# ReLU and row mean over 16384 rows: the last row in its own tile, and the program written with its own semaphores

## The chip, the cores and the metric

The kernel runs on one core of one Trainium2 chip. The metric is the device time of one execution in microseconds (us). The profile comes from one such execution. Engines are named as in the profile: DVE is VectorE, ACT is ScalarE, POOL is GpSimd, PE is TensorE (not used for work here), SP is SyncE, which issues the transfers. A letter q behind a name means the engine's sequencer, which handles waits and semaphores.

## The reference

The input x is float32 of shape 32 x 512 x 1024. Each value is replaced by max(x, 0), and the mean over the last axis is returned, as float32 of shape 32 x 512:

```python
relu_x = np.maximum(x, 0)
return np.mean(relu_x, axis=-1).astype(np.float32)
```

So there are 16384 rows of 1024 values. 67.11 MB are read and 64 KB are written.

## The kernel before

The rows are laid over the 128 partitions, 128 consecutive rows (index j from 0 to 127) to a partition. A tile `xt` holds 16 of a partition's rows: 64 KB per partition, 8 MB in all. The pool `in` has three such buffers. Seven full tiles are loaded with one transfer each (line 92). The eighth is loaded in smaller parts: row pieces of 8, 4, 2 and 1 rows (line 100), and then its last row, j = 127, in column pieces of 512, 256 and 256 columns (line 104). All transfers are issued by SP, and all go through one queue in that order.

The function `rows` gives each row to an engine: even rows to ACT, odd rows to DVE. `act_row` (line 15) is one activation with the function Relu, whose accumulated sum goes to a column of `sums`. `dve_row` (line 20) is one tensor_scalar, max with 0 and an accumulated sum; it can begin the sum with a value of its own (`init`). In the profile each of the two shows as two instructions, the main one and a read of the accumulator. `finish` (line 85) lets POOL multiply a range of `sums` by 1/1024 into `res`.

The end of the work is written out one by one. Row 126 (`prev`) is split in halves between ACT and DVE, and POOL joins and scales the two sums (line 118). The last row (`last`) lies in the same tile as the rest. Its first piece is split between ACT and DVE; POOL scales ACT's part (line 123). Its second piece is split likewise, where DVE's sum goes on from the one before (`init`), and ACT adds and scales its part (line 128). DVE alone takes the third piece, again going on from its sum, and then joins the two sides (line 132). SP stores `res` with one transfer (line 135).

The order on each engine is the order of the calls. What waits for what is worked out by the tile framework: it gives semaphores to engines and transfers, and eight of them are shared in turn by the transfers, so that a later transfer waits for the earlier one with the same semaphore. `tc.close()` (line 139) ends the tile context. At that place SP waits for the transfers' semaphores, all engines meet, POOL clears the semaphores, and all engines meet again. The function `issue_ahead_of_entry_barrier` then moves the first load in front of the meeting of all engines at the program's start (line 155 in the profile).

Of the kernel before, what the change touches and what calls it, by code (L numbers as in the profile page):

```python
# [1 line left out]

# [4 lines left out]

F32 = mybir.dt.float32
ALU = mybir.AluOpType
ACT = mybir.ActivationFunctionType  # L10


def act_row(nc, src, acc):

    nc.scalar.activation(out=src, in_=src, func=ACT.Relu, accum_out=acc)  # L15


def dve_row(nc, src, acc, init=None):

    nc.vector.tensor_scalar(  # L20
        out=src, in0=src, scalar1=0.0, scalar2=init,
        op0=ALU.max, op1=ALU.add, accum_out=acc,
    )


def issue_ahead_of_entry_barrier(nc):


    entry, body = nc.cur_f.blocks[0].instructions, None
    for block in nc.cur_f.blocks[1:]:  # L30
        for k, ins in enumerate(block.instructions):
            if ins.opcode == "DMACopy":
                body, load = block.instructions, k
                break
        if body is not None:
            break
    first = body[load]
    assert first.engine == mybir.EngineType.SP and not first.sync_info.on_wait
    assert all(i.opcode == "DMACopy" or i.engine != first.engine for i in body[:load])
    del body[load]  # L40
    at = next(k for k, i in enumerate(entry) if i.engine == first.engine and i.opcode == "Drain")
    entry.insert(at, first)


@with_exitstack
def kernel(
    ctx: ExitStack,
    tc: tile.TileContext,
    x: bass.AP,
    out: bass.AP,  # L50
):
    nc = tc.nc
    P = nc.NUM_PARTITIONS
    xf = x.flatten_outer_dims()
    R, D = xf.shape
    assert R % P == 0
    J = R // P
    inv = 1.0 / D
    xr = xf.rearrange("(p j) d -> p j d", p=P, j=J)
    outr = out.flatten().rearrange("(p j) -> p j", p=P, j=J)  # L60
    xlast = xr[:, J - 1, :]

    NB = 16
    full = J // NB - 1

    row_pieces = [8, 4, 2, 1]
    assert sum(row_pieces) == NB - 1
    col_pieces = [512, 256, 256]
    assert sum(col_pieces) == D

    pools = ctx.enter_context(ExitStack())
    in_pool = pools.enter_context(tc.tile_pool(name="in", bufs=3))
    res_pool = pools.enter_context(tc.tile_pool(name="res", bufs=1))
    sums = res_pool.tile([P, J], F32)
    res = res_pool.tile([P, J], F32)
    part = res_pool.tile([P, 10], F32)

    def rows(xt, lo, n, j0):

        for k in range(lo, lo + n):  # L80
            j = j0 + k
            (dve_row if j % 2 else act_row)(nc, xt[:, k, :], sums[:, j:j + 1])

    def finish(lo, hi):
        nc.gpsimd.tensor_scalar(  # L85
            out=res[:, lo:hi], in0=sums[:, lo:hi], scalar1=inv, scalar2=0.0, op0=ALU.mult, op1=ALU.add,
        )

    for t in range(full):
        j0 = t * NB  # L90
        xt = in_pool.tile([P, NB, D], F32, name="xt")
        nc.sync.dma_start(out=xt, in_=xr[:, j0:j0 + NB, :])  # L92
        rows(xt, 0, NB, j0)

    j0 = full * NB
    xt = in_pool.tile([P, NB, D], F32, name="xt")
    prev, last = xt[:, NB - 2, :], xt[:, NB - 1, :]
    lo = 0
    for n in row_pieces:
        nc.sync.dma_start(out=xt[:, lo:lo + n, :], in_=xr[:, j0 + lo:j0 + lo + n, :])  # L100
        lo += n
    c = 0
    for w in col_pieces:
        nc.sync.dma_start(out=last[:, c:c + w], in_=xlast[:, c:c + w])
        c += w

    finish(0, j0)
    lo = 0
    for n in row_pieces[:-1]:
        rows(xt, lo, n, j0)  # L110
        lo += n
    finish(j0, j0 + lo)

    act_row(nc, prev[:, :512], part[:, 0:1])
    dve_row(nc, prev[:, 512:], part[:, 1:2])
    nc.gpsimd.tensor_scalar(  # L118
        out=res[:, J - 2:J - 1], in0=part[:, 0:1], scalar1=part[:, 1:2], scalar2=inv, op0=ALU.add, op1=ALU.mult,
    )  # L120
    act_row(nc, last[:, :256], part[:, 2:3])
    dve_row(nc, last[:, 256:512], part[:, 3:4])
    nc.gpsimd.tensor_scalar(  # L123
        out=part[:, 4:5], in0=part[:, 2:3], scalar1=inv, scalar2=0.0, op0=ALU.mult, op1=ALU.add,
    )
    act_row(nc, last[:, 512:640], part[:, 5:6])
    dve_row(nc, last[:, 640:768], part[:, 6:7], init=part[:, 3:4])
    nc.scalar.activation(  # L128
        out=part[:, 7:8], in_=part[:, 5:6], func=ACT.Identity, scale=inv, bias=part[:, 4:5],
    )  # L130
    dve_row(nc, last[:, 768:], part[:, 8:9], init=part[:, 6:7])
    nc.vector.scalar_tensor_tensor(  # L132
        out=res[:, J - 1:J], in0=part[:, 8:9], scalar=inv, in1=part[:, 7:8], op0=ALU.mult, op1=ALU.add,
    )
    nc.sync.dma_start(out=outr, in_=res)

    pools.close()
    tc.close()
    tc.compile()
    issue_ahead_of_entry_barrier(nc)  # L140


# [1 line left out]
_INS = ['x']  # L144
_OUTS = [((32, 512), 'float32')]


# [23 lines left out]
```

## Time and profile before

| what | value |
|---|---|
| median of 20 runs | 164.0 us (163.61 to 164.39) |
| profiled execution, device time | 164.39 us |
| its span, first to last instruction | 162.6 us |
| DVE busy | 74.7 us (46%), 135 instructions |
| ACT busy | 69.6 us (43%), 134 instructions |
| POOL busy | 1.2 us (1%), 8 instructions |
| HBM read | 67.11 MB, 413 GB/s over the span |

The span runs from the first instruction of the kernel to its last, and the device time of the same execution is 1.79 us longer. The busy times are sums over the whole span. The waits of the sequencers and the transfers aren't in them, so the last few microseconds are read from the chain of waits and from the engines' timelines.

### The profile page before, as it was taken

The numbers are of one execution on the slowest core, as the hardware profiler recorded it, in microseconds if no ns is written. First come the engines' busy times: TensorE is split into PE (matmuls) and PEld (weight loads), VectorE is DVE, ScalarE is ACT, GpSimd is POOL, SyncE is SP. The second block draws the span as 40 slices with busy tenths as digits, with TensorE's granted clock in tenths as the row PEclk, the third lists the DMA queues.
The fourth block names the chain that finished last, engine by engine and source line by source line (L and its number), as shares of the span: only waits on it lengthen the run. The fifth ranks groups of instructions, "written<-read, shape, count | busy, mean of one in ns | idle before, by whom it ended". The sixth has DMA issues, their size and how long they took to land.

```text
span 162.6 us, 358 instructions
## 1 busy us (share of the span) xinstructions
DVE 74.7 (46%) x135; ACT 69.6 (43%) x134; POOL 1.2 (1%) x8
## 2 busy tenths in 40 slices
DVE  0000059700795009930099201990049800698993
ACT  3000059500793009910099001980049600696882
POOL 0000000000000000000000000000000000000001
DMA  7998997997998998998998998998999997999980
GB/s 258 516 468 355 468 516 322 451 516 339 435 516 355 419 516 371 403 468 387 435 486 373 435 484 371 435 500 371 419 500 419 403 484 339 427 435 403 407 310 17
DMA packets 2162, 67.19 MB, mean 413 GB/s; under 512 B 240, under 2 KB 624, under 8 KB 880
## 3 DMA queue, kind: packets, MB, share of 16 engines
q1 hardware_dynamic: 2160, 67.18, 96.4%
q14 instruction: 2, 0.02, 0.0%
HBM read 67.11 MB, written 0.07 MB: 413 GB/s over the span
## 4 chain that ended last, share of the span: by engine, by line
DMA 84%; DVE 13%; SPq 1%; issue 0%; DVEq 0%
DMA xt<-in_x_dram 84%; DVE xt L20 12%; SPq L100 1%; DVE res L132 0%; DVEq L20 0%; SPq L92 0%; DVEq L132 0%
## 5 line engine op out<-in xcount | busy, mean ns | idle before, releaser
L20 DVE TENSOR_SCALAR_CACHE_REDUCE xt<-xt 128x1024 f32<-128x1024 f32 (+1 forms) x65 | 73.6, 1194 | 85.2 <-DMA xt<-in_x_dram 84.9
L15 ACT ACTIVATE xt<-xt 128x1024 f32<-128x1024 f32 (+1 forms) x66 | 67.0, 1016 | 89.2 <-DMA xt<-in_x_dram 89.1
L15 ACT ACTIVATION_READ_ACCUMULATOR xt<-xt 128x1 f32 x66 | 12.3, 186 | 0.0
L20 DVE DVE_READ_ACCUMULATOR xt<-xt 128x1 f32 x65 | 5.3, 82 | 0.0
L85 POOL TENSOR_SCALAR res<-sums 128x112 f32<-128x112 f32 (+1 forms) x2 | 0.5, 252 | 157.2 <-DVE xt L20 157.2
L15 ACT ACT_TABLE_LOAD x1 | 1.3, 1283 | 0.8 <-PEq L155 0.8
L20 DVE TENSOR_SCALAR_CACHE_REDUCE xt<-xt,part 128x128 f32<-128x128 f32 (+1 forms) x2 | 0.8, 412 | 0.1
L128 ACT ACTIVATE part<-part 128x1 f32<-128x1 f32 x1 | 0.3, 294 | 0.1
L118 POOL TENSOR_SCALAR res<-part 128x1 f32<-128x1 f32 x1 | 0.3, 264 | 0.5 <-ACT xt L15 0.5
L132 DVE SCALAR_TENSOR_TENSOR res<-part 128x1 f32<-128x1 f32 x1 | 0.2, 160 | 0.1
L123 POOL TENSOR_SCALAR part<-part 128x1 f32<-128x1 f32 x1 | 0.2, 191 | 0.1
L20 DVE DVE_READ_ACCUMULATOR xt<-xt,part 128x1 f32 x2 | 0.2, 82 | 0.0
L155 POOL MEMSET const-bfloat16-1.0<- 128x1 bf16 x1 | 0.1, 101 | 0.0
L155 POOL MEMSET const-uint8-127<- 128x1 uint8 x1 | 0.1, 101 | 0.0
L155 POOL MEMSET const-float32-0.0<- 128x1 f32 x1 | 0.1, 98 | 0.2 <-issue 0.2
L155 POOL MEMSET const-float32-1.0<- 128x1 f32 x1 | 0.1, 98 | 0.0
## 6 DMA issues: line engine op xcount, KB each, us to landing
xt<-in_x_dram SPq DMA_DIRECT2D x1, 4096.0 KB, 39.0
xt<-in_x_dram SPq DMA_DIRECT2D x1, 2048.0 KB, 43.5
xt<-in_x_dram SPq DMA_DIRECT2D x1, 1024.0 KB, 45.5
xt<-in_x_dram SPq DMA_DIRECT2D x1, 512.0 KB, 46.4
xt<-in_x_dram SPq DMA_DIRECT2D x1, 256.0 KB, 46.5
xt<-in_x_dram SPq DMA_DIRECT2D x2, 128.0 KB, 42.7
xt<-in_x_dram SPq DMA_DIRECT2D x7, 49.4
out_dram<-res SPq DMA_DIRECT2D x1, 64.0 KB, 1.5
```

The source lines that it names most:

```text
L15: nc.scalar.activation(out=src, in_=src, func=ACT.Relu, accum_out=acc)
L20: nc.vector.tensor_scalar(out=src, in0=src, scalar1=0.0, scalar2=init, op0=ALU.max, op1=ALU.add, accum_out=acc,)
L85: nc.gpsimd.tensor_scalar(out=res[:, lo:hi], in0=sums[:, lo:hi], scalar1=inv, scalar2=0.0, op0=ALU.mult, op1=ALU.add,)
L100: nc.sync.dma_start(out=xt[:, lo:lo + n, :], in_=xr[:, j0 + lo:j0 + lo + n, :])
L118: nc.gpsimd.tensor_scalar(out=res[:, J - 2:J - 1], in0=part[:, 0:1], scalar1=part[:, 1:2], scalar2=inv, op0=ALU.add, op1=ALU.mult,)
L123: nc.gpsimd.tensor_scalar(out=part[:, 4:5], in0=part[:, 2:3], scalar1=inv, scalar2=0.0, op0=ALU.mult, op1=ALU.add,)
L128: nc.scalar.activation(out=part[:, 7:8], in_=part[:, 5:6], func=ACT.Identity, scale=inv, bias=part[:, 4:5],)
L132: nc.vector.scalar_tensor_tensor(out=res[:, J - 1:J], in0=part[:, 8:9], scalar=inv, in1=part[:, 7:8], op0=ALU.mult, op1=ALU.add,)
L155: nc = _bacc.Bacc("TRN2", target_bir_lowering=False, num_devices=1)
```

## The change

The program is no longer written within the tile framework. The tile context is closed at the top of the function, when it is still empty, so its two meetings of all engines stand at the start of the program. Buffers are allocated by name, and every wait and count is written by hand: each of the 14 loads has a semaphore of its own, and the engines count in three further ones (`act`, `dve`, `pool`). Loads, their sizes and their order are the same, and so is the work on rows 0 to 125. After the store SP clears the semaphores, waits for the store, and the program ends there.

Row 126 is split at column 448 instead of 512. The last row has a tile of its own with 1026 columns. ACT takes the whole first piece and writes its sum into column 1024; DVE takes the second piece and writes its sum into column 1025. One scalar_tensor_tensor on DVE then runs over columns 768 to 1025, that is the third piece and the two sums: max with 0, times 1/1024 from the tile `scale` (filled by POOL at the start), and the accumulated sum goes straight into `res`. The two sums aren't negative, so max leaves them as they are.

```diff
+    tc.close()
+    tc.compile()
...
+    last = sbuf("last", P, D + 2)
+    scale = sbuf("scale", P, D // 4 + 2)
+
+    loaded = [nc.alloc_semaphore(f"loaded{i}") for i in range(full + len(row_pieces) + len(col_pieces))]
+    act, dve, pool = (nc.alloc_semaphore(n) for n in ("act", "dve", "pool"))
+    stored = nc.alloc_semaphore("stored")
+
+    def load(i, dst, src):
+        nc.sync.dma_start(out=dst, in_=src).then_inc(loaded[i], 16)
+
+    def buf_free(t):
+        if t >= BUFS:
+            nc.sync.wait_ge(act, t - BUFS + 1)
+            nc.sync.wait_ge(dve, t - BUFS + 1)
+
+    for t in range(full):
+        buf_free(t)
+        load(t, bufs[t % BUFS][:, :, :], xr[:, t * NB:(t + 1) * NB, :])
...
+    nc.gpsimd.memset(scale[:, :], inv).then_inc(pool, 1)
+
+    def rows(i, xt, lo, n, j0):
+        nc.scalar.wait_ge(loaded[i], 16)
+        nc.vector.wait_ge(loaded[i], 16)
         for k in range(lo, lo + n):
             j = j0 + k
-            (dve_row if j % 2 else act_row)(nc, xt[:, k, :], sums[:, j:j + 1])
+            done = (dve_row if j % 2 else act_row)(nc, xt[:, k, :], sums[:, j:j + 1])
+            if k >= lo + n - 2:
+                done.then_inc(dve if j % 2 else act, 1)
...
-    act_row(nc, prev[:, :512], part[:, 0:1])
-    dve_row(nc, prev[:, 512:], part[:, 1:2])
+    nc.scalar.wait_ge(loaded[i], 16)
+    act_row(nc, prev[:, :448], part[:, 0:1]).then_inc(act, 1)
+    nc.vector.wait_ge(loaded[i], 16)
+    dve_row(nc, prev[:, 448:], part[:, 1:2]).then_inc(dve, 1)
...
-    act_row(nc, last[:, :256], part[:, 2:3])
-    dve_row(nc, last[:, 256:512], part[:, 3:4])
-    nc.gpsimd.tensor_scalar(
-        out=part[:, 4:5], in0=part[:, 2:3], scalar1=inv, scalar2=0.0, op0=ALU.mult, op1=ALU.add,
-    )
-    act_row(nc, last[:, 512:640], part[:, 5:6])
-    dve_row(nc, last[:, 640:768], part[:, 6:7], init=part[:, 3:4])
-    nc.scalar.activation(
-        out=part[:, 7:8], in_=part[:, 5:6], func=ACT.Identity, scale=inv, bias=part[:, 4:5],
-    )
-    dve_row(nc, last[:, 768:], part[:, 8:9], init=part[:, 6:7])
+    nc.scalar.wait_ge(loaded[i + 1], 16)
+    act_row(nc, last[:, :512], last[:, D:D + 1]).then_inc(act, 1)
+    nc.vector.wait_ge(loaded[i + 2], 16)
+    dve_row(nc, last[:, 512:768], last[:, D + 1:D + 2]).then_inc(dve, 1)
+    nc.vector.wait_ge(act, n_done + 1)
+    nc.vector.wait_ge(dve, n_done + 1)
+    nc.vector.wait_ge(loaded[i + 3], 16)
     nc.vector.scalar_tensor_tensor(
-        out=res[:, J - 1:J], in0=part[:, 8:9], scalar=inv, in1=part[:, 7:8], op0=ALU.mult, op1=ALU.add,
-    )
-    nc.sync.dma_start(out=outr, in_=res)
-
-    pools.close()
-    tc.close()
-    tc.compile()
+        out=last[:, 768:], in0=last[:, 768:], scalar=0.0, in1=scale[:, :], op0=ALU.max, op1=ALU.mult,
+        accum_out=res[:, J - 1:J],
+    ).then_inc(dve, 1)
+
+    nc.sync.wait_ge(pool, 2)
+    nc.sync.wait_ge(dve, n_done + 2)
+    nc.sync.dma_start(out=outr, in_=res[:, :]).then_inc(stored, 16)
+
+    nc.sync.sem_clear(range(used[0], used[-1] + 1))
+    nc.sync.wait_ge(stored, 16).then_inc(stored, -16)
```

In the built program the waits that stand directly in front of an instruction are merged into it as far as one wait fits; the rest stays as one wait instruction ahead of it. In front of the last DVE instruction that leaves one wait instruction (for the third piece and for DVE's own count) and one wait in the instruction itself (for ACT's count).

## The prediction

> **What bounds the kernel now.** I read the chain of waits first, because it says what the end waited for.
>
> ```profile
> DMA 84%; DVE 13%; SPq 1%; issue 0%; DVEq 0%
> DMA xt<-in_x_dram 84%; DVE xt L20 12%; SPq L100 1%; DVE res L132 0%; DVEq L20 0%; SPq L92 0%; DVEq L132 0%
> q1 hardware_dynamic: 2160, 67.18, 96.4%
> ```
>
> The load stream is the bound: its queue keeps the 16 DMA engines busy for 96.4% of the span, and the DVE steps inside the chain (two stretches of 9.21 us that free a buffer) are passed with two other tiles in flight. So an edit counts only if it moves the stream's start, the stream itself, or what follows its last byte. The end of the chain in order of time shows what follows:
>
> ```profile
> 111.48 46.36 DMA xt<-in_x_dram
> ...
> 157.86 1.07 DVE xt L20 x4
> 158.93 0.02 issue
> 158.96 0.23 DVE xt L20
> 159.18 0.04 issue
> 159.23 0.09 DVE xt L20
> 159.32 0.03 issue
> 159.34 0.50 DVE xt L20 x2
> 159.84 0.03 issue
> 159.87 0.02 DVEq L132
> 159.89 0.05 issue
> 159.94 0.16 DVE res L132
> ```
>
> Row 126 has landed at 157.84. From there five dependent DVE steps run to 160.10: half of row 126, three slices of the last row, one step that joins the halves. The last row's pieces were issued at 111.96, 112.44 and 120.11 and took 46.5, 46.4 and 39.0 us to land; the trace's landing events are 158.47, 158.81 and 159.13. DVE therefore ends 0.97 us after the last byte. What follows is on SP, in its waits:
>
> ```profile
> SPq L135 <- DVE res L132: 39.7, 1, 39.7
> SPq L139 <- DMA out_dram<-res: 1.1, 1, 1.1
> SPq L139 <- PEq L139: 0.6, 2, 0.4
> ```
>
> The store is issued at 160.17 and lands 1.55 us later, at 161.71. Then comes line 139, the exit of the tile context:
>
> ```profile
> L139 SPq EVENT_SEMAPHORE  x6: 17/28/28, 160.6 to 162.5; - x6
> L139 SPq DRAIN  x3: 7/7/7, 161.9 to 162.2; - x3
> L139 POOLq EVENT_SEMAPHORE_RANGE_CLEAR  x1: 95/95/95, 162.2 to 162.2; - x1
> ```
>
> SP checks its remaining DMA semaphores, all engines meet, POOL clears semaphores, all meet again; the last wait ends at 162.61, 0.90 us after the store landed. So three stages lie behind the stream: compute 0.97, store 1.61 with its 0.06 of hand-over, exit 0.90.
>
> [...]
>
> **The change, part by part.**
>
> *Start.* The first load stays ahead of the entry meeting. The exit's two meetings now stand before the remaining loads. The pair took 0.69 us at the end (161.92 to 162.61), so SP's second load moves from 0.77 to about 1.4 us and its third from 1.15 to about 1.9; ACT's 1.28 us table load, POOL's constant fill (new; I allow 1 us) and DVE's wait for it move likewise. The cover is the first 8 MB load, which lands at 22.33: cost nothing, 0.7 us without that cover.
>
> *Stream.* The seven tiles, four row pieces and three column pieces have the same sizes and order, all on SP's queue. Each load has its own semaphore, so the wait in front of the last column piece (7.2 us in SP's waits, to 120.11) is gone; that piece was still queued for 39 us, so it gains nothing. Buffers come free by the same two counts, issued at 31.6 to 110.2 as now, with the next tile already moving. Cost zero. [...] the streams keep nearly the same length (DVE 77 to 72 program instructions in the body), so two fetches stay. [...]
>
> *Row 126.* DVE takes 576 columns instead of 512. From 686 ns at 512 and 1215 at 1024 (1.03 ns a column) that is 752 ns, and the next instruction can start 75 ns before its end: 157.86 + 0.68 = 158.54. ACT takes 448: between 416 at 256 and 629 at 512 this is 576, free at 158.44. POOL's join (0.26 us) follows by about 159.0, and only SP's store waits for it.
>
> *Last row.* ACT takes the whole first piece (512): lands 158.47, starts 158.49, 629 ns, its accumulator read ends 94 ns after (as at 158.40 + 0.19 now), at 159.21. DVE takes the second piece (256): lands 158.81, starts 158.84, 420 ns, read over at 159.26. Then DVE waits for ACT's sum, for its own and for the third piece (159.13). Line 132 now started 0.112 us after the sum before it was written, through one extra wait instruction; the changed program has one there too: start 159.37. Behind it on DVE is nothing, and SP waits for it.
>
> *The final instruction*, 258 columns with accumulation. [...] I take 0.43: the one-source rows with accumulation run at 1.03 ns a column[...]. Its accumulator read adds 10 ns beyond its end: 159.81. It replaces the two slices with their chained starts, ACT's and POOL's scaling, and the join.
>
> *Store.* SP starts 0.064 us after (160.103 to 160.167 now): 159.87 instead of 160.17, a gain of 0.29 us. Landing 1.55 later: 161.42.
>
> *Exit.* SP clears the semaphores during the store's flight (POOL's clear took 95 ns; the cover is about 1.1 us; without it 0.1 us) and waits for the store: 0.016 until the wait sees it, 0.028 for the wait. End 161.46. Gain here 0.85 us.
>
> Sum: 162.61 − 0.29 − 0.85 = 161.46, so −1.15 us. The profiled execution was 164.39 in all, 1.79 more than its span; with that kept it becomes 163.24. It was the slowest of the 20 runs; the same saving from the median gives 164.0 − 1.15 = **162.85 us**. A difference of 0.2%, 0.33 us, is about what a measurement of this kernel can tell from none.
>
> **Rivals.**
>
> *The final instruction at half throughput.* [...] It costs 0.27: 163.12.
>
> *More than I count.* The 1.79 us outside the span shrink, since four engines leave early and only SP comes last, or the instruction fetches fall on a DMA engine with slack. Worth about 0.35: 162.50. Against: whatever waits for all engines still waits for SP.
>
> *The exit meeting isn't really removed.* [...] only the 0.29 of the tail is left: 163.71, just inside 0.2%. For: [...] the time outside the span isn't in the profile. [...] This is also the case in which the change doesn't do what it says.
>
> *Slower.* The last row's new tile starts at an SBUF address that is a multiple of 32 but not of 64 bytes, by the built program; the old rows started on multiples of 64. If such writes are slow, all packets of the last three pieces are: per engine 8 of 84 ns and 16 of 46 ns, 1.41 us. The final instruction has 0.18 us of slack on the third piece, so at r times the cost the end moves by 1.41(r−1) − 0.18. It cancels the gain at r = 1.94 and is slower by 0.2% from r = 2.2; at 2.4, say, 164.6. Against: packets here cost 8 ns plus 38 ns a KB from 1 KB to 64 KB, with no trace of an edge penalty.
>
> **How the numbers follow.** Main case 0.60, half throughput 0.13, more than counted 0.09, exit repaid 0.10, slower 0.08. The first three are faster by over 0.2%: 0.82; within 0.10; slower 0.08. The range takes in those three, 162.50 to 163.12, with 0.2 below and, for medians that differ between sets and a fetch on the wrong engine, 0.4 above: 162.3 to 163.5, with 0.18 left out.
>
> **What would show it.** Right: a span of about 161.5; no meetings after the store; the last instruction is SP's wait, some 0.05 us behind the landing; the final DVE instruction at about 0.43 us, starting about 0.11 us after DVE's second-piece sum; the third piece still landing 1.3 us after row 126; second load near 1.4 us and the first tile's landing unmoved. Wrong: a final instruction near 0.7; third piece later than 1.5 us after row 126; a span shorter by 1.15 with the time unmoved, which would mean the time outside the span grew; or a lower stream rate between 20 and 140 us.

## The result, and the profile after

The changed kernel takes 162.38 us (median, 162.03 to 162.58) against 163.95 us of the kernel before (median, 163.61 to 164.39). The ratio is 0.9902, with a 95% interval of 0.9892 to 0.9912. The change makes the kernel faster by 1.57 us, about 1%. The forecast was 162.85 us within 162.3 to 163.5.

The profiled execution took 162.53 us, its span 161.19 us. So two things became shorter: the span, by 1.42 us against the profiled execution of before (162.61), and the time outside the span, from 1.78 to 1.34 us. Over several executions of each kernel the same split shows with less chance in it (35 of the kernel before, beside the first experiment, and 8 of the changed kernel; spans are on record to 0.1 us):

| median over the executions | kernel before | changed kernel | difference |
|---|---|---|---|
| span | 162.10 us (161.8 to 162.6) | 161.05 us (160.7 to 161.2) | 1.05 |
| device time less span | 1.79 us (1.74 to 1.84) | 1.34 us (1.28 to 1.39) | 0.45 |

The load stream is still the bound. These are lines of the page of the changed kernel; the lower two have packets, MB and the share of the 16 DMA engines.

```profile
span 161.2 us, 336 instructions
...
q1 hardware_dynamic: 2160, 67.18, 97.3%
q14 instruction: 2, 0.02, 0.0%
```

The chain that ended last says little here: on this page it holds only the final DVE instruction. The last event of the program is now SP's own wait for the store, and the chain loses its thread there. The DVE timeline (start, length, then the instruction) shows the end of the compute:

```profile
157.59 0.75 DVE L20 TENSOR_SCALAR_CACHE_REDUCE rows<-rows 128x576 f32<-128x576 f32 x1
158.27 0.08 DVE L20 DVE_READ_ACCUMULATOR rows<-rows 128x1 f32 x1
158.58 0.42 DVE L20 TENSOR_SCALAR_CACHE_REDUCE last<-last 128x256 f32<-128x256 f32 x1 [0.23 <-DMA last<-in_x_dram]
158.93 0.08 DVE L20 DVE_READ_ACCUMULATOR last<-last 128x1 f32 x1
159.11 0.43 DVE L165 SCALAR_TENSOR_TENSOR last<-last,scale 128x258 f32<-128x258 f32 x1
159.46 0.08 DVE L165 DVE_READ_ACCUMULATOR last<-last,scale 128x1 f32 x1
```

DVE is done with its part of row 126 before the second piece has landed and idles for 0.23 us in front of it. The final instruction takes 0.43 us and starts 0.10 us after the sum of the second piece is written (159.01). ACT's timeline shows the first piece, whose sum is ready before that:

```profile
158.23 0.63 ACT L15 ACTIVATE last<-last 128x512 f32<-128x512 f32 x1
158.77 0.19 ACT L15 ACTIVATION_READ_ACCUMULATOR last<-last 128x1 f32 x1
```

The third piece landed at 158.89 (by the trace's landing events), so DVE ended 0.65 us behind the last byte, where the old chain needed 0.97. What follows is in SP's waits:

```profile
SPq L172 <- DVE last L165: 46.5, 1, 46.5
SPq L178 <- SPq L178: 1.1, 1, 1.1
SPq L55 <- PEq L55: 0.5, 2, 0.3
```

The store goes out at 159.62 and lands at 161.16; SP's wait for it (line 178) ends at 161.19, and so does the program. The two meetings of line 55 are at the start now: SP's last wait in them ends at 1.36 us, and its second load goes out at 1.42. The first tile landed at 22.31 (22.33 before).

From the last landing to the end of the span it was 162.61 − 159.13 = 3.48 us before and is 161.19 − 158.89 = 2.30 us now. The difference, 1.17 us before rounding, stands against the 1.15 of the forecast. That the last byte came 0.24 us earlier in this execution is left for the first experiment.

### The profile page after: what moved, and what is told of

It reads as the page before. It is cut to its first block, busy times and chain, and to the rows that moved or that the text cites. A ratio compares the mean times of both kernels' runs of the same rounds, so it can differ in the third digit from the quotient of the medians.

```text
span 161.2 us, 336 instructions
## 1 busy us (share of the span) xinstructions
DVE 74.3 (46%) x132; ACT 69.2 (43%) x131; POOL 1.3 (1%) x8
## 5 line engine op out<-in xcount | busy, mean ns | idle before, releaser
L20 DVE TENSOR_SCALAR_CACHE_REDUCE rows<-rows 128x1024 f32<-128x1024 f32 x64 | 73.4, 1208 | 84.9 <-DMA rows<-in_x_dram 84.7
L15 ACT ACTIVATE rows<-rows 128x1024 f32<-128x1024 f32 x64 | 66.2, 1036 | 88.3 <-DMA rows<-in_x_dram 88.2
L15 ACT ACTIVATION_READ_ACCUMULATOR rows<-rows 128x1 f32 x64 | 12.0, 187 | 0.0
L20 DVE DVE_READ_ACCUMULATOR rows<-rows 128x1 f32 x64 | 5.3, 83 | 0.0
L15 ACT ACTIVATE last<-last 128x512 f32<-128x512 f32 x1 | 0.6, 630 | 0.0
```

What stands on the lines that cost most here:

```text
L15: return nc.scalar.activation(out=src, in_=src, func=ACT.Relu, accum_out=acc)
L20: return nc.vector.tensor_scalar(out=src, in0=src, scalar1=0.0, scalar2=init, op0=ALU.max, op1=ALU.add, accum_out=acc,)
```

## The experiments

My theory after the result: three separate savings, the tail (0.29 us), the exit within the span (0.85) and 0.45 outside the span, which comes from four engines leaving early. The rivals: the last saving belongs to the tail, or to something else in the exit; or the stream itself became faster. Each experiment had the kernel before run beside it. "Outside" is the device time less the span, the median over the executions.

### The kernel before once more

No edit.

> The kernel before once more, for the spans of several of its executions. Both theories: 163.95. If the 0.24 us by which the last piece landed earlier in the changed kernel's trace (158.89 against 159.13) is chance, spans here scatter from about 161.9 to 162.6 around 162.2, and the last landing lies around 158.9. If the hand-written program makes the stream itself faster, the spans stay at 162.5 or more. The time outside the span should be 1.79 in each execution.

Measured: 163.86 us, ratio 1.0000 (0.9991 to 1.0009), spans of 161.8 to 162.5 with a median of 162.10, outside 1.77. In the profiled execution, of 162.1 us, the last piece landed at 158.61, not 159.13. So the profiled execution of before had a late stream by chance, and the 0.24 us aren't owed to the change. Its trace shows where it fell behind: eight 64 KB packets that start between 64.7 and 65.6 us took 2.9 to 3.2 us instead of 2.42. What slowed them is open. The forecast, which took its steps from that execution and its saving from the median, was not harmed by it.

### The new tail alone

The kernel before, within the tile framework and with its exit, but with the new end of the work:

```diff
+    last = res_pool.tile([P, D + 2], F32)
+    scale = res_pool.tile([P, D // 4 + 2], F32)
+    nc.gpsimd.memset(scale, inv)
...
+    act_row(nc, last[:, :512], last[:, D:D + 1])
+    dve_row(nc, last[:, 512:768], last[:, D + 1:D + 2])
+    nc.vector.scalar_tensor_tensor(
+        out=last[:, 768:], in0=last[:, 768:], scalar=0.0, in1=scale, op0=ALU.max, op1=ALU.mult,
+        accum_out=res[:, J - 1:J],
+    )
```

> The kernel before with only the new end of the work: row 126 split at 448, the last row in its own tile, one final DVE instruction; still within the tile framework, with its exit. My theory (three separate savings: tail, exit, outside): 0.22 to 0.29 us less, since the final instruction gets two further waits here, so about 163.7 with 1.79 outside the span. Rival (the new tail is what shortens the time outside the span too, because ACT and POOL stop earlier): about 163.25.

Measured: 163.60 us, ratio 0.9985 (0.9977 to 0.9993), so 0.28 us less; outside 1.79, as before. The DVE timeline of this kernel shows where a part of the saving stays behind:

```profile
158.50 0.08 DVE L20 DVE_READ_ACCUMULATOR last<-last 128x1 f32 x1
158.79 0.43 DVE L126 SCALAR_TENSOR_TENSOR last<-last,scale 128x258 f32<-128x258 f32 x1 [0.21 <-DVE last L20]
```

The framework puts two wait instructions in front of the final instruction, and it starts 0.21 us after the sum before it, twice what one wait instruction takes in the changed kernel. From the last landing (158.46) to the end of the span it is 3.26 us, against 3.48: a saving of 0.21 us before rounding. With the waits of the changed kernel (0.10 us in place of 0.21) it would be 0.11 more. The tail is worth what the forecast gave it, and the rival that ties the outside time to it falls.

### The new program alone

The changed program with the old end of the work, waits written by hand:

```diff
-    last = sbuf("last", P, D + 2)
+    last = xt[:, NB - 1, :]
...
+    act_row(nc, last[:, :256], part[:, 2:3]).then_inc(act, 1)
+    dve_row(nc, last[:, 256:512], part[:, 3:4]).then_inc(dve, 1)
...
+    dve_row(nc, last[:, 640:768], part[:, 6:7], init=part[:, 3:4]).then_inc(dve, 1)
...
+    dve_row(nc, last[:, 768:], part[:, 8:9], init=part[:, 6:7]).then_inc(dve, 1)
```

> The changed program with the old end of the work: row 126 split at 512, the last row in its 8 MB tile and in slices, ACT's and POOL's scaling and the join. My theory: the exit's 0.85 us in the span and 0.45 outside it go, the tail stays: 163.95 - 1.30 = 162.65, with 1.34 outside. Rival (the outside saving belongs to the tail): 163.1 with 1.79 outside.

Measured: 162.79 us, ratio 0.9932 (0.9917 to 0.9947), so 1.09 us less; outside 1.35, span median 161.45. The outside saving comes with the program. Within the span the saving is 0.65 us, less than the 0.85 of the exit. The end of the old chain in this kernel's DVE timeline shows one reason:

```profile
159.06 0.08 DVE L20 DVE_READ_ACCUMULATOR rows<-rows,part 128x1 f32 x1
159.27 0.48 DVE L20 TENSOR_SCALAR_CACHE_REDUCE rows<-rows,part 128x256 f32<-128x256 f32 x1
159.67 0.08 DVE L20 DVE_READ_ACCUMULATOR rows<-rows,part 128x1 f32 x1
159.79 0.16 DVE L181 SCALAR_TENSOR_TENSOR res<-part 128x1 f32<-128x1 f32 x1
```

These are the lines of the kernel before for the same two steps:

```profile
159.23 0.08 DVE L20 DVE_READ_ACCUMULATOR xt<-xt,part 128x1 f32 x1
159.34 0.48 DVE L20 TENSOR_SCALAR_CACHE_REDUCE xt<-xt,part 128x256 f32<-128x256 f32 x1
```

The third piece had landed at 158.87, and the chain ends 1.07 us later (0.97 in the kernel before). The slice of 256 starts 0.13 us after the sum before it is written (159.14), where the kernel before needed 0.04 (159.31 to 159.34); the slice ahead of it lost the same. There the wait for DVE's own sum, which comes last, stood in the DVE instruction, and the wait for the transfer in a wait instruction ahead of it, which took 21 ns and ended before the sum was written (at 158.86 and 159.18, the sums at 158.92 and 159.31). My hand-written order puts them the other way round, and the two slices start later by 0.09 to 0.10 us each. The changed kernel's trace shows the steps of such a start: the wait instruction in front of the final instruction ends 0.05 us after the sum of the second piece is written (159.06 against 159.01), and the final instruction starts 0.05 us behind that. The join gets 0.08 of this back: it starts 0.04 us after the sum before it, where the kernel before needed 0.11. The other 0.1 us of the 0.2 lies ahead of the last landing: from there to the end of the span it is 161.60 − 158.87 = 2.73 us, 0.75 less than before, which is the 0.85 without those 0.10.

The parts' gains are 0.28 and 1.09, together 1.37 of the 1.57 us. The missing 0.2 us are what the waits of the two kernels cost. From the last landing to the end the traces show savings of 0.21 us for the tail and 0.75 for the program. Add the 0.11 of the second wait instruction and the 0.10 of the order of the waits, and it is the 1.17 us of the changed kernel. The medians of the kernel before differ by 0.1 us between the sets (163.81 to 163.95), so the sums of times say no more than this.

### All five engines leave together

```diff
     nc.sync.wait_ge(stored, 16).then_inc(stored, -16)
+    nc.all_engine_barrier()
```

> The changed kernel with one meeting of all engines added behind SP's wait for the store, so that all five engines leave together. My theory (the time outside the span shrank because four engines leave early and have their share of the closing work done before SP comes): span longer by the meeting, 0.33 to 0.40, and the time outside back at about 1.79: 162.38 + 0.37 + 0.45 = 163.2. Rival (the outside time depends on something else, for instance on the branch to a closing block or on the semaphores' clearing): outside stays at 1.34, 162.75.

Measured: 162.92 us, ratio 0.9940 (0.9925 to 0.9956), outside 1.79. The time outside the span is back. These are three of the waits and drains of the added line in that kernel (count, then shortest, median and longest in ns, first and last start in us):

```profile
L179 POOLq EVENT_SEMAPHORE  x2: 17/17/17, 161.2 to 161.3; - x2
L179 PEldq DRAIN  x1: 8/8/8, 1.5 to 1.5; - x1
...
L179 PEldq EVENT_SEMAPHORE  x1: 51/51/51, 161.4 to 161.4; - x1
```

The meeting itself took only 0.27 us in the span (161.13 to 161.40), not 0.33 to 0.40: the engines had reported long before, as PE's drain at 1.5 us shows, so only SP's report and the release are left. The sum of the steps, 161.05 + 0.27 + 1.79, would be 163.11; the spans of this set came out 0.2 us shorter, which is within the scatter of the stream between sets.

### One engine leaves late

Four kernels, each with one engine that waits until SP has seen the store land (the engine is named in the list `late`; here it is DVE):

```diff
+    late = [(e, nc.alloc_semaphore(f"late{k}")) for k, e in enumerate((nc.vector,))]
...
     nc.sync.wait_ge(stored, 16).then_inc(stored, -16)
+    for e, s in late:
+        nc.sync.sem_inc(s, 1)
+        e.wait_ge(s, 1).then_inc(s, -1)
```

> The changed kernel with POOL alone made to wait until SP has seen the store land, so POOL and SP leave together, ACT, DVE and PE early. The meeting of all five (late_all) brought the time outside the span from 1.34 back to 1.79. If any engine that leaves late has its own closing work to do (the same for each): about 1.79 here too. If one engine's closing work is the long one, 1.79 appears for that engine alone and 1.34 to 1.4 for the others. The span grows by at most 0.1 (SP's signal and POOL's wait).

> The same with PE alone made late. Same closing work for each engine: about 1.79 outside the span. One long engine: 1.79 if it is PE, else 1.34 to 1.4. PE's waits took 51 ns against 17 to 21 of the others in the end of the kernel before, so if one is long I take PE.

> The same with ACT alone made late. Same closing work for each engine: about 1.79 outside the span. One long engine: 1.79 if it is ACT, else 1.34 to 1.4.

> The changed kernel with DVE alone made late, to complete the list (outside the span: SP alone 1.34, ACT late 1.52, PE late 1.64, POOL late 1.87). If each engine has its own closing stretch, DVE shows a value of its own; SP leaves 0.1 us before it, so a value of 1.24 would mean that DVE's is no longer than SP's, and anything above 1.87 can't be, since in the kernel before DVE leaves after POOL and the end comes 1.8 us later. If the theory is wrong and what counts is how late the last engine of any kind leaves, DVE's value equals ACT's, 1.52.

| last to leave | device time less span | the same in the profiled execution, span unrounded | time | ratio |
|---|---|---|---|---|
| SP (changed kernel) | 1.34 us (1.28 to 1.39) | 1.34 us | 162.38 us | 0.9902 (0.9892 to 0.9912) |
| DVE | 1.46 us (1.42 to 1.47) | 1.46 us | 162.44 us | 0.9915 (0.9887 to 0.9942) |
| ACT | 1.52 us (1.50 to 1.54) | 1.50 us | 162.43 us | 0.9911 (0.9895 to 0.9928) |
| PE | 1.64 us (1.61 to 1.70) | 1.66 us | 162.78 us | 0.9929 (0.9914 to 0.9944) |
| POOL | 1.87 us (1.84 to 1.90) | 1.88 us | 162.85 us | 0.9933 (0.9918 to 0.9948) |

Neither of the two outcomes that I had set down for the first three came: it is not the same for each engine, and not one long engine among equal ones. Each engine has its own stretch between its last instruction and the end, and POOL's is the longest, 1.87 us. (The figures also hold whatever of the device time lies ahead of the first instruction. The five kernels start alike, so their differences are shown, and the absolute lengths are not.) POOL's figure explains the kernels in which all leave together: in the meeting of all five POOL's last instruction ends 0.09 us before the span, and 1.87 − 0.09 = 1.78; in the kernel before POOL's last instruction ends at 162.52, and the profiled execution took 164.39, again 1.87. So by these figures the kernel before was ended by POOL leaving its exit, and the changed one by SP, whose stretch is 0.53 us shorter. What the engines do in that stretch is not in the trace.

### The store on ACT

```diff
-    nc.sync.dma_start(out=outr, in_=res[:, :]).then_inc(stored, 16)
+    nc.scalar.dma_start(out=outr, in_=res[:, :]).then_inc(stored, 16)
```

and likewise the waits for it and the clearing.

> The changed kernel with the store, the clearing and the wait for the store on ACT in SP's place, so ACT leaves last and SP early. With ACT late beside SP the time outside the span was 1.52 against 1.34. If each engine has its own closing stretch and the one that leaves last sets the end (SP 1.34, ACT 1.52, PE 1.64, POOL 1.87), 1.52 here and about 162.55 in all. If what counts is how many engines leave late, one here, 1.34 and about 162.4.

Measured: outside 1.54 (1.54 to 1.55), and 1.51 in the profiled execution with its span unrounded, which is ACT's figure. So it is which engine leaves last that counts, not how many are late. The time was 162.35 us, ratio 0.9915 (0.9901 to 0.9930), because the spans came out at 160.8; their scatter between sets is as large as the 0.2 us in question.

### Fewer instructions

All loads stay, but of each of the first ten only the last two rows are summed, so this kernel leaves out most of the work. The wide DVE instruction is there for its length alone.

```diff
+    nc.gpsimd.memset(sums[:, :], 0.0)
...
-        for k in range(lo, lo + n):
+        for k in range(lo + n - 2, lo + n):
...
+    nc.vector.scalar_tensor_tensor(
+        out=bufs[0][:, 0, :], in0=bufs[0][:, 0, :], scalar=0.0, in1=bufs[0][:, 1, :], op0=ALU.max, op1=ALU.mult,
+        accum_out=sums[:, 0:1],
+    )
```

> The changed kernel with all loads, but only the last two rows of each of the first ten loads summed (the other columns of sums stay at the 0 that POOL writes), so ACT and DVE have some 100 instructions less each and should need no further instruction fetch; and one DVE scalar_tensor_tensor over two SBUF rows of 1024 float32 with accumulation while DVE idles. My theory (each of the two 8 KB fetches in the stream holds up one DMA engine, and the last one sets the landing): no instruction packets within the span, first and last landing of the last piece less than 1.1 us apart against 1.4, spans 0.2 to 0.5 below 161.05. Rival (the lag between the DMA engines has other causes, such as their staggered start): 1.3 to 1.5 apart, span unchanged. [...]

Measured: 161.87 us, ratio 0.9879 (0.9864 to 0.9893), span median 160.50, 0.55 below the changed kernel's. The two ran in different sets; against the kernel before beside it this one saves 2.03 us where the changed kernel saves 1.57, so 0.46 more (0.38 by the ratios). The page has no line for the instruction queue any more, and the packet count is down by the two:

```profile
DMA packets 2160, 67.18 MB, mean 418 GB/s; under 512 B 240, under 2 KB 624, under 8 KB 880
...
q1 hardware_dynamic: 2160, 67.18, 97.4%
```

A load's landing shows in the trace as 16 events. Call the time from the first to the last of them its lag. The lag of the last piece is 0.77 us here (157.42 to 158.20), against 1.41 in the changed kernel (157.48 to 158.89). The edit also takes more than four fifths of ACT's and DVE's work away (from 20 to 140 us DVE is busy for 9.7 us in place of 56.0, ACT for 9.3 in place of 51.3), so these two traces alone leave a rival. The lags of the loads before it settle most of that:

| kernel | fetches at | lag of the third, fourth and fifth load | lag of the last piece |
|---|---|---|---|
| changed kernel | 65.0 and 65.3 us | 0.95, 1.51, 1.51 us | 1.41 us |
| kernel before once more | 86.6 and 86.8 us | 0.66, 0.74, 1.20 us | 1.10 us |
| store on ACT | 67.3 and 67.3 us | 0.98, 0.99, 0.99 us | 0.91 us |
| fewer instructions | none | 0.85, 0.86, 0.84 us | 0.77 us |

These loads land at about 61, 81 and 100 us. In twelve of the thirteen traces with fetches the lag steps up by 0.22 to 0.55 us at the load in which a fetch falls, be it the fourth or the fifth, and keeps nearly all of it to the end, while ACT and DVE do the same work throughout. In the thirteenth, with the store on ACT, there is no step. No other lag rises by more than 0.21 us, but for the 0.56 us of the eight slow packets in the first trace of the kernel before. Behind the two fetches of the changed kernel one 64 KB packet each took 2.7 and 3.0 us, where the usual one takes 2.42.

So in these traces a part of the stream is held up where a fetch falls, by 0.22 to 0.55 us in twelve of the thirteen, and what it costs differs from one execution to the next. The 0.69 us between the last landings of the changed kernel and of this one are at the upper end: in eight other traces of the changed program the last piece lands at 158.41 to 158.87. That the part held up is the one DMA engine that carries the fetch would fit, but is not shown, since the trace doesn't name the engines. For a kernel that must sum all rows this saving isn't to be had by this edit.

The wide instruction, by its source line in this kernel:

```profile
L140 DVE SCALAR_TENSOR_TENSOR rows<-rows x1: 1225/1225/1225, 22.4 to 22.4; 128x1024 f32<-128x1024 f32 x1
```

The one-source rows of this width took 1215 ns in the kernel before (the mean of 63), so the form with two sources took 10 ns more here, not twice the time.

### The store in two

```diff
-    nc.sync.wait_ge(pool, 2)
+    nc.sync.wait_ge(pool, 3)
+    nc.sync.dma_start(out=outr[:, :J - 2], in_=res[:, :J - 2]).then_inc(early, 16)
+    nc.sync.wait_ge(pool, 4)
     nc.sync.wait_ge(dve, n_done + 2)
-    nc.sync.dma_start(out=outr, in_=res[:, :]).then_inc(stored, 16)
+    nc.sync.dma_start(out=outr[:, J - 2:], in_=res[:, J - 2:]).then_inc(stored, 16)
...
+    nc.sync.wait_ge(early, 16).then_inc(early, -16)
```

> The changed kernel with the store in two: 126 columns as soon as POOL has scaled them (about 157.9), the last two columns when the final DVE instruction is done. The first store should run just as the stream ends. If the store's 1.55 us is in part the moving of 512 bytes per partition (its packets took 27 ns each, eight to a DMA engine), the second store lands 0.1 to 0.2 us sooner after its issue and the time falls to about 162.25. If it is all issue and confirmation, it stays within 0.05 of 162.38. If pieces of 8 bytes are slow to write, or the first store delays the last loads, it is longer than 162.5.

Measured: 161.95 us, ratio 0.9887 (0.9870 to 0.9903), outside 1.33. The two stores among the transfers of this kernel, with their size and the time to landing:

```profile
out_dram<-res SPq DMA_DIRECT2D x1, 63.0 KB, 1.5
out_dram<-res SPq DMA_DIRECT2D x1, 1.0 KB, 1.4
```

The small store landed 1.41 us after its issue (159.28 to 160.69), the whole one 1.54 (159.62 to 161.16). That accounts for 0.13 us of the 0.43 between the medians, and so does the whole stretch from the last landing to the end, 2.17 us against 2.30. Some 0.14 more is the set: the kernel before ran at 163.81 there and at 163.95 beside the changed kernel. The intervals of the two ratios overlap, and the two kernels did not run side by side. It is the quickest version here that computes everything, by its median; that it beats the changed kernel is likely by the trace and not settled by the times.

### The first load behind the meetings

```diff
-    issue_ahead_of_entry_barrier(nc)
```

> The changed kernel without the step that puts the first load ahead of the meetings. SP's next load stood at 1.42 in the changed kernel's trace, behind three meetings. My theory (the three meetings cost nothing only because the first load runs beside them): the stream starts some 1.3 us later and the time is about 163.7. Rival (the meetings are short enough not to matter, or the stream catches up): at most 162.8.

Measured: 163.51 us, ratio 0.9986 (0.9978 to 0.9993). That is 1.13 us more than the changed kernel by the medians; but this kernel saves 0.30 us against the kernel before beside it where the changed kernel saves 1.57, so 1.27 us are lost. SP's timeline of this kernel, three loads merged:

```profile
1.39 1.31 SPq L93 DMA_DIRECT2D rows<-in_x_dram  x3
```

The same line of the changed kernel:

```profile
0.00 2.36 SPq L93 DMA_DIRECT2D rows<-in_x_dram  x3
```

The stream starts 1.39 us later, the last piece lands 1.32 us later (160.21 against 158.89), and so nearly all of it reaches the end. In this kernel the meetings at the start are free only behind the first load, as the forecast had it.

## Why the prediction was right, and where it was off

**The sign and the span: right, by the forecast's own steps.** From the last landing to the end of the span 1.17 us were saved against 1.15 forecast, and the medians of the spans differ by 1.05. The tail and the exit are each borne out by a kernel that has only the one.

| step | forecast | measured |
|---|---|---|
| SP's second load, behind the meetings | about 1.4 us | 1.42 us, first tile unmoved |
| row 126 on DVE, 576 columns | 752 ns | 753 ns |
| row 126 on ACT, 448 columns | 576 ns | 577 ns |
| third piece after row 126 | 1.3 us | 1.33 us (157.56 to 158.89) |
| final instruction | 0.43 us | 0.428 us |
| its start after the sum before it | 0.11 us | 0.10 us |
| store to landing | 1.55 us | 1.54 us |
| landing to the end | 0.04 us | 0.034 us |

**The time outside the span: the step that was mis-sized.** The forecast kept 1.79 us; it became 1.34, and those 0.45 us are nearly the whole 0.47 by which 162.85 was above 162.38. The argument that failed stands among the rivals: "whatever waits for all engines still waits for SP". It took the closing work for one common wait. The runs with one late engine show five stretches of different length, and an end set by the engine whose leaving and stretch together come last. The rival "more than I count" had the right direction, the right reason (four engines leave early) and about the right size (0.35), at 0.09. The range held, since it had been drawn 0.2 us below that rival; 162.38 lies 0.08 us above its lower end, so that it held is in part luck.

**The rivals.** Half throughput of the final instruction didn't come: 428 ns at 258 columns and 1225 at 1024 make 1.04 ns a column, against the 1.03 of the one-source rows on which the forecast's 0.43 us rested. The 0.27 us set down for it, about 1.03 ns more for each of the 258 columns, were the author's estimate; no trace showed such a case. The exit repaid outside the span didn't come either: the time there went down, from 1.79 to 1.34 us. The slow writes into the last row's own tile didn't come: packets of 1 KB and 2 KB took 46 and 84 ns (medians) in both traces.

**The store: the length was right.** It took 1.54 us where 1.55 were forecast. In the trace of the kernel before the first packet starts 0.84 us after the store's issue begins, the packets take 0.35, and the landing comes 0.35 after the last of them. So more than half of it lies ahead of the data here, and less than a quarter behind. The sum didn't depend on this division, since it took the whole 1.55 as measured.

**The instruction fetches.** The forecast kept two, and two there were, 8 KB each, but at 65 us in place of the 85 to 87 in the trace of the kernel before. What its range allowed for where they fall was the author's estimate. Measured are the steps of the lag, from 0.01 to 0.55 us, and the run without them, which also leaves out most of the work on the rows and saves some 0.4 to 0.5 us more than the changed kernel.

## What to carry to other kernels

In a stream-bound kernel read the end in three parts: from the last landing to the store's issue, the store, and the exit; then look at the time outside the span as a fourth, which depends on which engine leaves last. Put meetings behind the first load (ahead of it they cost 1.27 us here), and let the engine that has to wait for the last store leave alone, with POOL long gone (1.34 us outside the span for SP alone, 1.87 with POOL late). A last step that takes earlier sums as further columns of its own input can replace a chain of small instructions, which in the kernel before started 0.04 to 0.11 us after the sums before them; of two waits, the one that is satisfied last belongs in the instruction itself (0.04 us here, against 0.10 to 0.13).

## What the runs showed that I had not expected

- The engines differ in the time from their last instruction to the end of the execution. With whatever lies ahead of the first instruction it is 1.34 us for SP, 1.46 for DVE, 1.52 for ACT, 1.64 for PE and 1.87 for POOL.
- A meeting of all engines to which four had long reported took 0.27 us, and its price outside the span (0.45 us) was larger than that.
- Two 8 KB instruction fetches, 0.02% of the bytes, widened the lag between the first and the last landing of every later load by 0.22 to 0.55 us in twelve of thirteen traces.
- Of two waits in front of a DVE instruction, the late one cost 0.04 us where it stood in the instruction and 0.10 to 0.13 where it stood in the wait instruction ahead. The changed kernel's final instruction has its late wait, for DVE's own sum, in the wait instruction; turning the two round was not tried.
- A store of 8 bytes per partition landed only 0.13 us sooner than one of 512 (1.41 us after its issue against 1.54); in both, the first packet started 0.84 to 0.85 us after the issue began.
